# Hymba block on one core: the second half's gate in turn with the first attention's first steps, and two changes to the order of loads

## The chip, the core and the metric

The kernel runs on one core of a Trainium2 chip. The metric is the device time of one execution in microseconds (us): 2039.54 us as the median of three executions of the kernel before (2036.24, 2039.54 and 2040.94). The engines named below are TensorE (PE: matrix products and transposes; its weight loads are listed apart as PEld), VectorE (DVE: adds, subtractions, scans, multiplications), ScalarE (ACT: copies and functions such as exp), GpSimd (POOL, hardly used here) and SyncE (SP), whose queue issues nearly all of the transfers (DMAs) between device memory and the core's own memory.

## The reference

The block has 2048 positions of width 1024. One projection makes the inputs of two mixers: gated linear attention with four heads (key width 64, value width 128) and a short convolution of width 3 over 512 columns. Their outputs are joined, projected and added to the input; a feed-forward part of inner width 2816 follows, with a normalisation ahead of each part and at the end. Cut to what matters here:

```python
proj = rmsnorm(x, norm1_g) @ w_in
p_q, p_k, p_v, p_g, p_a, c_b, c_c, c_h = split(proj)
log_a = log_sigmoid(p_a @ w_gate_up + b_gate) / 16          # the gate
# attention, chunk by chunk (b is the running sum of log_a in the chunk)
scores  = where(causal, (q * exp(b)) @ (k * exp(-b)).T, 0)
o       = scores @ v + (q * exp(b)) @ state
state   = exp(b_last) * state + (k * exp(b_last - b)).T @ v
o_gla   = rmsnorm(o, gla_norm_g) * silu(p_g)
o_conv  = c_b * causal_depthwise_conv(c_c * c_h, conv_w)
x = x + concat([o_gla, o_conv]) @ w_out
x = x + (silu(h2 @ w_ffn_gate) * (h2 @ w_ffn_up)) @ w_ffn_down    # h2 = rmsnorm(x, norm2_g)
return rmsnorm(x, norm_f_g)
```

## The kernel before

**Tiling.** The sequence is cut into four blocks `b` of 512 positions, two to a half (half 0: blocks 0 and 1). The kernel's attention chunk `t` has 128 positions, so there are four to a block and eight to a half. Tiles are 128 partitions by 512 elements of f32 in most places.

**Products.** Large products go by units. A unit (`unit`) makes a 2x2 group of output tiles from a 2x2 group of weight quarters with seven products in place of eight, in the manner of Strassen and Winograd; `S1` to `S4` are sums and differences of the weight quarters `A11`, `A12`, `A21`, `A22`, and `B11`, `T1` and so on are those of the operands. Each number is split into a high part and a low part: `split` makes the high part on ACT (line 206) and the low part on DVE (line 207). `product_step` then issues three matmuls per step: high by high (line 504), high by low (505) and low by high (506), and four or eight steps make a product. `plus` (line 538, on DVE) adds a finished product to an output tile, `copied` (line 550, on ACT) copies one out of PSUM. `all_plus` is the list of all of these adds so far.

**Weights.** A unit's raw weights come in one load of 1 MB (`raw`), into one of two buffers. `unit_weights` makes the sums at line 456. The first three units of the second half use `weights_in_step` instead: its sums stand at lines 482 (`s1 = a21 + a22`), 483 and 484 (which leaves `S2` in the raw tile), each held behind an earlier `plus`. The raw buffer is free for the next unit's load when its last quarter has been split.

**Order of stages.** `in_proj(0)`, `in_proj(1)` (twelve units), `first_out_proj` (the out projection of the first half, in four pairs of output rows `d0`, ten adds to a pair), `out_proj` (that of the second half), then the feed-forward part by halves. In `first_out_proj` the loads that the second half's out projection needs are issued as well; `build_mix` (line 1411) loads convolution outputs (`s_mix`, shown as `op` from `sm`, by `load_whole`) and attention outputs (`op` from `sgla`).

**Background.** Smaller work is written as generators whose steps lie between the products. After each product `tick` (line 284) is called: it takes one background step at every other call, and with `hasty` set one more at a call in four. `hastened(steps, n)` sets `hasty` for the first `n` steps, `chain` takes generators one after the other, and `in_turn(one, *others)` (line 297) takes a step of the others, then a step of `one`, and so on, and at the end the rest of `one`.

**The gate.** `gate(1, ops)` has five steps. The first makes the low-rank logits (32 matmuls, line 1028) and stacks them; each of the other four makes one tile `z` (two matmuls, line 1054) and runs `forget_gate` on it: four activations, one DVE operation (line 1067), four scans of 128 elements (line 1070), and DVE and ACT work after them (lines 1073 to 1076). Its result is stored to device memory (`s_d`).

**The attention.** `gla_half(half)` (line 1129) runs the eight chunks. `gla_fetch` (line 1155) issues the loads `kq` (queries and keys, 256 KB), `ee` (decays, 128 KB, from `s_d`), `vt` and `gt`. `gla_scaled` makes two exponentials of the decays on ACT (lines 1163 and 1164) and multiplies queries and keys by them on DVE (1165 and 1166). `gla_scores` makes the scores on PE (line 1176), masks them on DVE (1179) and transposes keys and values (1182 and 1185). `gla_outputs` and `gla_finish` follow one step later (`o_ps`, `kv`, and the transpose `ot` at line 1251). The loads for chunk n+1 are issued after the scores of chunk n. `gla_half(0)` runs during `in_proj(1)`; `gla_half(1)` begins there in the last units and runs on in `first_out_proj`.

**What sets the order.** Each engine runs its instructions in the order in which they were issued to it, and waits at an instruction whose inputs are not there; all behind it on that engine wait too. The order within an engine is settled when the program is built. `behind(marks)` makes the instructions inside it stand behind the mark in that order. SP's queue issues its DMAs in order as well.

Of the kernel before, what the change touches and what calls it, by code (L numbers as in the profile page):

```python
# [11 lines left out]
F32 = mybir.dt.float32  # L12
# [15 lines left out]
HEADS = 4  # L28
# [26 lines left out]
def tile_hymba_block(ctx, tc, x, xt, win, wa, wgu, wout, wffn, wdown, wdown_first, small, out):  # L55
# [57 lines left out]
    def by_chunks(name, n):  # L113
        return [dram.tile([P, PT, n, P], F32, name=f"{name}{b}") for b in range(NB)]

    s_kq, s_d, s_v, s_g = [
        by_chunks(name, n) for name, n in (("sk", 4), ("sd", 2), ("sv", 4), ("sg", 4))
    ]
    s_x1 = scratch("sx", KD)
    s_mix = [  # L120
        [dram.tile([P, PB], F32, name=f"sm{b}_{k}") for k in range(4)] for b in range(NB)
    ]
# [24 lines left out]
    def bank(name="mm"):  # L147
        return ps.tile([P, PB], F32, name=name, tag="mm")
# [4 lines left out]
    def bt(name, shape=(P, PB)):  # L153
        return bx[0].tile(list(shape), F32, name=name, tag="b")

    def load(dst, src):
        return nc.sync.dma_start(dst, src)
# [10 lines left out]
    all_plus = []  # L168

    @contextmanager  # L170
    def behind(marks):

        with ExitStack() as stack:
            for m in marks:
                stack.enter_context(tc.issue_after(m.ins))
            yield
# [26 lines left out]
    def split(src, hi, lo):  # L203
        if ordered:
            return split_in_order(src, hi, lo)
        last_hi[:] = [act.activation(hi, src, AF.Copy)]  # L206
        last_lo[:] = [dve.tensor_tensor(lo, src, hi.bitcast(F32), ALU.subtract)]  # L207
        return last_lo[0]
# [64 lines left out]
    background = []  # L273
# [23 lines left out]
    def in_turn(one, *others):  # L297

        for other in others:
            for _ in other:  # L300
                yield
                if next(one, True) is None:
                    yield
        yield from one
# [6 lines left out]
    def pause(n):  # L311
        for _ in range(n):
            yield

    def hastened(steps, n):
        hasty.append(True)
        for i, _ in enumerate(steps):
            if i == n:
                hasty.clear()
            yield  # L320
# [669 lines left out]
    def load_undivided(src):  # L990
        o = opp.tile([P, 2, PB], F32R, name="op", tag="op")
        load(o[:, 1, :].bitcast(F32), src[:])
        return o

    def load_whole(src):

        o = load_undivided(src)
        split(o[:, 1, :].bitcast(F32), o[:, 0, :], o[:, 1, :])
        return o

    def load_pair(src):
        o = opp.tile([P, 2, PB], F32R, name="op", tag="op")
        load(o[:].bitcast(F32), src[:])
        return o
# [11 lines left out]
    def gate(half, ops, mark=None):  # L1016

        a = bank("a_ps")  # L1020
        names = "B11", "T1", "B21", "B22"
        with behind([mark] if mark else []):
            for n in names:
                for k in range(4):
                    q = {"B11": 3 * k + 1, "T1": 3 * k, "B21": 2 * k + 13, "B22": 2 * k + 12}[n]
                    w = wa_sb[:, 32 * q : 32 * q + P]
                    for e in range(2):
                        pe.matmul(  # L1028
                            a[:], w, ops[n][k][:, e, :],
                            start=(n, k, e) == ("B11", 0, 0),  # L1030
                            stop=n == "B22" and k == 3 and e == 1, skip_group_check=True,
                        )
        if mark:
            yield

        stacks = []
        if half == 0:
            second_factor()
        for j in range(2):
            stack = bx[0].tile([96, PB], F32R, name="a_sb", tag="b")  # L1040
            r, low = [slice(32 * n, 32 * n + 32) for n in (j, 1 - j)]
            with behind(held):
                act.activation(stack[r, :], a[r, :], AF.Copy)
                act.activation(stack[64:96, :], a[r, :], AF.Copy)
                dve.tensor_tensor(stack[low, :], a[r, :], stack[r, :].bitcast(F32), ALU.subtract)
            stacks.append(stack)
        yield
        for j in range(2):
            small = decays[2 * half + j] = [
                mtiny.tile([P, 2, PT], F32, name=n, tag=n, bufs=4) for n in ("em", "dn", "el")  # L1050
            ]
            for i in range(2):
                z = bank("z")
                pe.matmul(
                    z[:], wgu_sb[:, i * P : (i + 1) * P], stacks[j][:], start=True, stop=True
                )
                forget_gate(2 * half + j, i, z, *small)
                yield
# [69 lines left out]
    def gla_half(half):  # L1128
        chunks = [(b, t) for b in (2 * half, 2 * half + 1) for t in range(PT)]
        with tc.issue_after(last_silu[0].ins):  # L1130
            tables = act.preload_act_table_set("natural_log_exp_and_others")
        fetched = gla_fetch(*chunks[0])
        yield
        with tc.issue_after(tables.ins):
            cur = gla_scaled(*fetched)
        yield
        o = None
        for n, (b, t) in enumerate(chunks):
            s = gla_scores(b, t, *cur)
            yield  # L1140
            if n + 1 < len(chunks):
                fetched = gla_fetch(*chunks[n + 1])
            if o is not None:
                yield from gla_finish(*chunks[n - 1], *o)
            o = gla_outputs(b, t, *s)
            if n + 1 < len(chunks):
                cur = gla_scaled(*fetched)
            yield
        yield from gla_finish(b, t, *o)
        done.add((b, t))  # L1150
        yield
# [3 lines left out]

    def gla_fetch(b, t):
        kq, e, vt, g = [bt(n, (P, 4, P)) for n in ("kq", "ee", "vt", "gt")]
        for dst, src in ((kq[:], s_kq), (e[:, 2:4, :], s_d), (vt[:], s_v), (g[:], s_g)):
            load(dst, src[b][:, t])
        return kq, e, vt, g  # L1160

# [250 lines left out]
    def build_mix():  # L1412
        def pair(b, k):
            if k < HEADS:
                return load_pair(s_gla[b][:, k])
            with behind(all_plus[-4:-3] if k < HEADS + 2 else all_plus[-2:-1]):
                return load_whole(s_mix[b][k - HEADS])

        return {k: [pair(2 + j, k) for j in range(2)] for k in LATE_HEADS}

# [411 lines left out]
    ops, raw, between, steps, rest = opening()  # L1832
# [7 lines left out]
    drain_background()  # L1840
    ops = load_pairs(s_h1)
    ahead.append(conv_operands())
    background.extend([pause(3), hastened(chain(gate(1, ops), gla_half(0)), 12)])
    in_proj(1, ops)
    drain_background(lambda: (1, PT - 1) in done)
    ssq = first_out_proj(residual(0), *mix_operands())
# [118 lines left out]
```

## Time and profile before

| | |
|---|---|
| median of three executions | 2039.54 us |
| profiled execution, its own time | 2035.4 us |
| its span (first to last instruction) | 2033.6 us |
| mean granted TensorE clock | 0.996 |
| PE busy | 2011.0 us, 99% of the span |
| DVE busy | 1566.0 us, 77% |
| ACT busy | 973.5 us, 48% |
| moved by DMA | 425.12 MB, 209 GB/s over the span |

The profiled execution is one of its own, 4.1 us under the median. Its span is the time between the first and the last instruction on the core; 1.8 us of its time lie outside. "Busy" is the share of the span in which an engine had an instruction under way, and the granted clock is the share of full TensorE speed that the chip allowed. A view by windows gives the busy time of each engine in one stretch, and the number of its instructions in brackets; the view of waits sums, for each pair of lines, the time in which one engine stood idle until the other was done; the timeline lists instructions with their start and length. Names of tiles are shown in the profile without their buffer numbers; the listing of the program's order in the next section has them, so that one tile can be followed.

### The profile page before, as it was taken

The numbers are of one execution on the slowest core, as the hardware profiler recorded it, in microseconds if no ns is written. First come the engines' busy times: TensorE is split into PE (matmuls) and PEld (weight loads), VectorE is DVE, ScalarE is ACT, GpSimd is POOL, SyncE is SP. The second block draws the span as 40 slices with busy tenths as digits, with TensorE's granted clock in tenths as the row PEclk, the third lists the DMA queues.
The fourth block names the chain that finished last, engine by engine and source line by source line (L and its number), as shares of the span: only waits on it lengthen the run. The fifth ranks groups of instructions, "written<-read, shape, count | busy, mean of one in ns | idle before, by whom it ended". The sixth has DMA issues, their size and how long they took to land.

```text
span 2033.6 us, 26792 instructions
## 1 busy us (share of the span) xinstructions
PE 2011.0 (99%) x9275; PEld 1654.9 (81%) x9275; DVE 1566.0 (77%) x2837; ACT 973.5 (48%) x1941; POOL 10.3 (1%) x17
## 2 busy tenths in 40 slices
PE   9999999999989999999999999999999999999998
PEld 8788887788878888888888888887888888888886
DVE  7878868677867877777777688887767767778886
ACT  6664465754544444444444552334434444454345
POOL 0000000000000000000000000000000000000001
PEclk9999999999999999999999999999999999999999
DMA  7366876654786863545545676486444434486653
GB/s 264 119 202 218 289 262 210 187 171 137 261 296 219 297 239 130 181 158 210 181 154 183 226 282 253 185 288 263 168 157 171 169 137 171 179 329 222 248 217 130
DMA packets 191943, 425.12 MB, mean 209 GB/s; under 512 B 17760, under 2 KB 67136, under 8 KB 182336
## 3 DMA queue, kind: packets, MB, share of 16 engines
q1 hardware_dynamic: 191088, 422.76, 59.1%
q8 instruction: 73, 1.20, 0.2%
q10 hardware_dynamic: 720, 0.66, 0.1%
q14 instruction: 62, 0.51, 0.1%
HBM read 277.60 MB, written 145.75 MB: 208 GB/s over the span
## 4 chain that ended last, share of the span: by engine, by line
PE 95%; DMA 3%; ACT 1%; DVE 1%; issue 0%; SPq 0%; POOL 0%; POOLq 0%; ACTq 0%
PE mm L504 27%; PE mm L506 27%; PE mm L505 27%; PE mm L1431 1%; PE mm L1434 1%; PE mm L1432 1%; PE mm L1393 1%; DMA op<-shT 1%; PE a_ps L1028 1%; PE mm L809 1%; PE mm L811 1%; PE mm L810 1%; PE mm L1751 1%; PE mm L1399 1%; PE o_ps L1201 1%; DMA op<-sgla 0%
## 5 line engine op out<-in xcount | busy, mean ns | idle before, releaser
L504 PE MATMUL mm<-op,wq 128*128 128x512 f32 x2499 | 973.2, 392 | 2.5 <-ACT c L550 1.2
L505 PE MATMUL mm<-op,wq 128*128 128x512 f32 x2499 | 971.8, 390 | 0.3 <-DVE op L207 0.2
L506 PE MATMUL mm<-op,wq 128*128 128x512 f32 x2499 | 961.1, 390 | 2.4 <-DVE wq L207 2.1
L206 ACT ACTIVATE wq<-raw 128x512 fp32r<-128x512 f32 (+2 forms) x628 | 361.5, 580 | 591.2 <-PE mm L506 490.8
L504 PEld LDWEIGHTS mm<-op,wq 128*128 128x128 f32 x2499 | 469.1, 188 | 104.8 <-ACT wq L206 2.4
L506 PEld LDWEIGHTS mm<-op,wq 128*128 128x128 f32 x2499 | 469.2, 188 | 101.8 <-DVE wq L207 4.1
L505 PEld LDWEIGHTS mm<-op,wq 128*128 128x128 f32 x2499 | 469.3, 188 | 97.4 <-DVE op L207 2.0
L207 DVE TENSOR_TENSOR wq<-raw,wq 128x512 fp32r<-128x512 f32 (+2 forms) x628 | 390.8, 627 | 145.4 <-ACT wq L206 144.1
L538 DVE TENSOR_TENSOR c<-mm,c 128x512 f32<-128x512 f32 x196 | 135.0, 689 | 75.5 <-PE mm L506 70.6
L538 DVE TENSOR_TENSOR y<-mm,y 128x512 f32<-128x512 f32 x185 | 126.9, 688 | 51.4 <-PE mm L506 50.7
L550 ACT ACTIVATE c<-mm 128x512 f32<-128x512 f32 x198 | 115.6, 589 | 29.5 <-PE mm L506 27.0
L456 DVE TENSOR_TENSOR raw<-raw 128x512 f32<-128x512 f32 (+2 forms) x190 | 117.0, 621 | 2.1
L206 ACT ACTIVATE wq<-s 128x512 fp32r<-128x512 f32 (+2 forms) x100 | 58.0, 580 | 110.2 <-PE mm L506 95.7
L456 DVE TENSOR_TENSOR s<-raw 128x512 f32<-128x512 f32 (+2 forms) x95 | 59.1, 622 | 31.7 <-DMA raw<-in_wffn_dram 20.8
L207 DVE TENSOR_TENSOR op<-op 128x512 fp32r<-128x512 f32 x108 | 71.1, 686 | 3.1 <-ACT op L206 3.0
L206 ACT ACTIVATE op<-op 128x512 fp32r<-128x512 f32 x108 | 63.1, 621 | 8.6 <-DMA op<-sa_T 3.5
L207 DVE TENSOR_TENSOR wq<-s,wq 128x512 fp32r<-128x512 f32 (+2 forms) x100 | 62.5, 625 | 1.8 <-ACT wq L206 1.0
L456 DVE TENSOR_TENSOR raw<-s,raw 128x512 f32<-128x512 f32 (+2 forms) x95 | 59.2, 623 | 1.3
L605 ACT ACTIVATE sg<-mm 128x512 f32<-128x512 f32 x26 | 15.5, 598 | 87.6 <-PE mm L506 87.6
L605 ACT ACTIVATE c<-c 128x512 f32<-128x512 f32 x78 | 48.9, 629 | 13.1 <-DVE c L538 10.4
L1431 PE MATMUL mm<-op,wq 128*128 128x512 f32 x128 | 50.0, 392 | 0.0
L1432 PE MATMUL mm<-op,wq 128*128 128x512 f32 x128 | 49.8, 389 | 0.0
(238 smaller groups left out, 1666.4 us busy)
## 6 DMA issues: line engine op xcount, KB each, us to landing
raw<-in_wffn_dram SPq DMA_DIRECT2D x44, 1024.0 KB, 6.6
sa_B<-so SPq DMA_DIRECT2D x47, 512.0 KB, 3.6
op<-sa_B SPq DMA_DIRECT2D x47, 512.0 KB, 6.6
raw<-in_win_dram SPq DMA_DIRECT2D x22, 1024.0 KB, 6.0
sa_T<-so SPq DMA_DIRECT2D x44, 512.0 KB, 4.3
op<-sa_T SPq DMA_DIRECT2D x44, 512.0 KB, 6.7
raw<-in_wdown_dram SPq DMA_DIRECT2D x24, 768.0 KB, 5.5
sx<-y SPq DMA_DIRECT2D x48, 256.0 KB, 3.7
```

Source lines behind the costliest of these rows:

```text
L206: last_hi[:] = [act.activation(hi, src, AF.Copy)]
L207: last_lo[:] = [dve.tensor_tensor(lo, src, hi.bitcast(F32), ALU.subtract)]
L456: dve.tensor_tensor(*args)
L504: pe.matmul(o[:], wh, xh, start=first and k == 0, stop=False, skip_group_check=True)
L505: pe.matmul(o[:], wh, xl, start=False, stop=False, skip_group_check=True)
L506: return pe.matmul(o[:], wl, xh, start=False, stop=k == n - 1, skip_group_check=True)
L538: last_plus[:] = [dve.tensor_tensor(t[:], o[:], t[:], ALU.add)]
L550: last_out[:] = [act.activation(t[:], o[:], AF.Copy)]
L605: last_silu[:] = [act.activation(s[:], c[:], AF.Silu)]
L809: pe.matmul(acc[:], wq[:, 0, c], p[:, 0, :], start=first, stop=False)
L1431: pe.matmul(o[e, j][:], wh, m[:, 0, :], start=n == 0, stop=False)
L1432: pe.matmul(o[e, j][:], wh, m[:, 1, :], start=False, stop=False)
```

## The change

There are three edits. The steps of the second half's gate and the first steps of the first half's attention are taken in turn instead of one after the other. In `gla_fetch` the decays are loaded ahead of the queries and keys. In `build_mix` the load of a convolution output is put behind the add that lies twenty adds back (two pairs of rows), and its split stays behind the add that it was behind before.

```diff
     def gla_fetch(b, t):
         kq, e, vt, g = [bt(n, (P, 4, P)) for n in ("kq", "ee", "vt", "gt")]
-        for dst, src in ((kq[:], s_kq), (e[:, 2:4, :], s_d), (vt[:], s_v), (g[:], s_g)):
+        for dst, src in ((e[:, 2:4, :], s_d), (kq[:], s_kq), (vt[:], s_v), (g[:], s_g)):
             load(dst, src[b][:, t])
         return kq, e, vt, g
...
                 return load_pair(s_gla[b][:, k])
+            with behind(all_plus[-20:-19]):
+                o = load_undivided(s_mix[b][k - HEADS])
             with behind(all_plus[-4:-3] if k < HEADS + 2 else all_plus[-2:-1]):
-                return load_whole(s_mix[b][k - HEADS])
+                split(o[:, 1, :].bitcast(F32), o[:, 0, :], o[:, 1, :])
+            return o
...
-    background.extend([pause(3), hastened(chain(gate(1, ops), gla_half(0)), 12)])
+    background.extend([pause(3), hastened(in_turn(gla_half(0), gate(1, ops)), 12)])
     in_proj(1, ops)
```

What this does to the order of the instructions shows at three places. The first is DVE in the first units of the second half, before the change, around the low part of the second unit's `S2` (`raw_3243` are that unit's weights, `wq_3255` its `S2`; `g1` and `g2` are tiles of four different runs of `forget_gate`):

```order
L484 TENSOR_TENSOR raw_3243<-s1_3245,raw_3243 128x512
L1067 SCALAR_TENSOR_TENSOR g2_3200<-g2_3200,g1_3199 128x512
L1166 SCALAR_TENSOR_TENSOR kq_3229<-kq_3229,ee_3230 128x256
L1074 TENSOR_TENSOR g2_3082<-g1_3081 128x512
L1074 TENSOR_TENSOR g2_3117<-g1_3116 128x512
L1070 SCALAR_TENSOR_TENSOR g1_3168<-ones_92,g2_3169 128x128 x4
L456 TENSOR_TENSOR s1_3479<-raw_3480 128x512
L1070 SCALAR_TENSOR_TENSOR g1_3199<-ones_92,g2_3200 128x128 x4
L207 TENSOR_TENSOR wq_3255<-raw_3243,wq_3255 128x512
L207 TENSOR_TENSOR wq_3258<-raw_3243,wq_3258 128x512
```

The same place after the change (the unit's weights are `raw_3226` now, and its `S2` is `wq_3238`):

```order
L1074 TENSOR_TENSOR g2_3174<-g1_3173 128x512
L1179 COPY_PREDICATED scores_106<-mask_94,sc_3203 128x2x128
L483 TENSOR_TENSOR raw_3226<-raw_3226 128x512
L207 TENSOR_TENSOR wq_3235<-s1_3228,wq_3235 128x512
L1076 TENSOR_TENSOR dn_3103<-em_3102,el_3104 128x4
L484 TENSOR_TENSOR raw_3226<-s1_3228,raw_3226 128x512
L456 TENSOR_TENSOR s1_3479<-raw_3480 128x512
L207 TENSOR_TENSOR wq_3238<-raw_3226,wq_3238 128x512
```

Between the row of line 484 and the low part of `S2` (line 207) there stood eight scans, two differences of line 1074 and three further operations; now one sum of the next unit's weights stands there.

The second place is DVE some products later, around the add `c22` of the same unit, before the change:

```order
L207 TENSOR_TENSOR wq_3482<-raw_3480,wq_3482 128x512
L1236 TENSOR_SCALAR hsq_3371<-hsq_3371 128x4
L456 TENSOR_TENSOR raw_3480<-s1_3479,raw_3480 128x512
L538 TENSOR_TENSOR c22_3297<-mm_3261,c22_3297 128x512
L218 TENSOR_TENSOR hl_3372<-hy_3373 128x4
L207 TENSOR_TENSOR wq_3488<-s1_3479,wq_3488 128x512
```

And after it:

```order
L207 TENSOR_TENSOR wq_3482<-raw_3480,wq_3482 128x512
L456 TENSOR_TENSOR raw_3480<-s1_3479,raw_3480 128x512
L1067 SCALAR_TENSOR_TENSOR g2_3377<-g2_3377,g1_3376 128x512
L1070 SCALAR_TENSOR_TENSOR g1_3376<-ones_92,g2_3377 128x128 x4
L1165 TENSOR_TENSOR kq_3459<-kq_3459,ee_3460 128x256
L1166 SCALAR_TENSOR_TENSOR kq_3459<-kq_3459,ee_3460 128x256
L538 TENSOR_TENSOR c22_3297<-mm_3244,c22_3297 128x512
L1074 TENSOR_TENSOR g2_3377<-g1_3376 128x512
L207 TENSOR_TENSOR wq_3488<-s1_3479,wq_3488 128x512
```

The last gate tile's operation of line 1067 and its four scans, and the two multiplications of the third chunk (number 2, `kq_3459` with its decays `ee_3460`), which wait for that chunk's loads, now stand ahead of the add.

The third place is SP's queue at the first rows of the first half's out projection, as the difference between the two programs (`sk`, `sd`, `sv` and `sg` are the stored keys and queries, decays, values and output gates; `sm` the stored convolution outputs; `sgla` the attention's):

```order
 L157 DMA y_5832<-in_xt_dram 128x512
 L163 DMA sm2_3_172<-c11_5110 128x512
+L157 DMA ee_5748<-sd3_120 128x256
 L157 DMA kq_5747<-sk3_116 128x512
-L157 DMA ee_5748<-sd3_120 128x256
 L157 DMA vt_5749<-sv3_124 128x512
 L157 DMA raw_5937<-in_wout_dram 128x2048
 L163 DMA sgla2_193<-gt_5266 512x1x128
 L157 DMA gt_5750<-sg3_128 128x512
```

The decays have moved one place forward, past the queries and keys, and nothing else in the piece has moved. The loads `op` from `sm` stand in front of it and behind it, at the same places as before. The edit in `build_mix` taken alone moves no row on any engine: its mark is an add on DVE, and the load is an instruction of SP's queue.

## The prediction

> **What bounds the kernel now.** I read first the page's head and its engines' busy time, then the waits of PE, then the chain of waits around each large one, then the timeline of each engine and the windows there.
>
> ```profile
> span 2033.6 us, 26792 instructions
> PE 2011.0 (99%) x9275; PEld 1654.9 (81%) x9275; DVE 1566.0 (77%) x2837; ACT 973.5 (48%) x1941; POOL 10.3 (1%) x17
> ...
> PE sc L1176 <- DVE kq L1166: 6.2, 1, 6.2
> PE rb_ps L1719 <- ACT rep L1710: 2.3, 2, 1.7
> PE mm L506 <- DVE wq L207: 2.1, 1, 2.1
> ```
>
> The columns of the last three rows are the sum, the count and the longest of the waits. TensorE bounds the kernel: only 2033.6 − 2011.0 = 22.6 us of the span is left in which it stands. The change takes no matmul away and adds none, so it can win only from those 22.6 us, or from the clock. Two single waits, 6.2 and 2.1 us, are the largest; the change moves work near both. The third row lies in the feed-forward part, which the change leaves alone.
>
> The 2.1 us lie in the second half's first units:
>
> ```profile
> 308.34 0.39 PE L505 MATMUL mm<-op,wq 128*128 128x512 f32 x1
> 308.72 0.50 PE L506 MATMUL mm<-op,wq 128*128 128x512 f32 x1
> ...
> 315.80 0.50 PE L506 MATMUL mm<-op,wq 128*128 128x512 f32 x1 [2.14 <-DVE wq L207]
> ...
> 309.18 0.69 DVE L484 TENSOR_TENSOR raw<-s,raw 128x512 f32<-128x512 f32 x1
> ...
> 311.93 1.37 DVE L1070 TENSOR_TENSOR_SCAN g<-ones,g 128x128 f32<-128x128 f32 x4
> ...
> 313.79 1.37 DVE L1070 TENSOR_TENSOR_SCAN g<-ones,g 128x128 f32<-128x128 f32 x4
> 315.07 1.87 DVE L207 TENSOR_TENSOR wq<-raw,wq 128x512 fp32r<-128x512 f32 x3
> ...
> 309.91 1.68 ACT L206 ACTIVATE wq<-raw 128x512 fp32r<-128x512 f32 x3 [0.51 <-DVE raw L484]
> ...
> 313.00:316.00 3.00, 0.86 (x5) 0.43 (x4) 3.00 (x8) 1.18 (x4) 0.00 (x0) 1.00 0.94 224
> ```
>
> `S2` is ready at 309.87 on DVE, and its high part starts on ACT at 309.91; a third of that row's 1.68 us makes it ready at about 310.5. Its low part starts only at 315.07: DVE is busy for all of the 3 us of the window with what stands ahead of it, eight of the gate's scans among it. PE's next low weight is that tile. The last row is a window: each engine's busy time with its instructions in brackets (PE, PEld, DVE, ACT, POOL), then the granted clock, the DMA share and GB/s. The clock stays at 1.00, so the gap costs its length and no more.
>
> The 6.2 us lie where the first half's out projection starts its pairs, at the scores of a later chunk:
>
> ```profile
> 571.00 0.61 PE L1399 MATMUL mm<-op,wq 128*128 128x512 f32 x2
> 577.78 1.22 PE L1176 MATMUL sc<-kq 64*128 64x128 f32 x8 [6.17 <-DVE kq L1166]
> ...
> 570.31 0.32 SPq L157 DMA_DIRECT2D kq<-sk  x1
> 570.92 0.32 SPq L157 DMA_DIRECT2D ee<-sd  x1
> ...
> kq<-sk SPq DMA_DIRECT2D x1, 256.0 KB, 5.2
> ...
> ee<-sd SPq DMA_DIRECT2D x1, 128.0 KB, 5.5
> ...
> 576.40 0.42 ACT L1163 ACTIVATE ee<-ee 128x256 f32<-128x256 f32 x1 [0.72 <-DMA ee<-sd]
> 576.85 0.42 ACT L1164 ACTIVATE ee<-ee 128x256 f32<-128x256 f32 x1
> ...
> 576.85 0.43 DVE L1165 TENSOR_TENSOR kq<-kq,ee 128x256 f32<-128x256 f32 x1 [1.23 <-ACT ee L1163]
> 577.30 0.42 DVE L1166 SCALAR_TENSOR_TENSOR kq<-kq,ee 128x256 f32<-128x256 f32 x1
> ...
> 540.00:571.00 31.00, 31.00 (x177) 25.20 (x176) 25.50 (x62) 13.45 (x44) 0.00 (x0) 1.00 1.03 397
> 571.00:578.00 7.00, 0.83 (x5) 0.41 (x5) 4.62 (x11) 4.47 (x10) 0.00 (x0) 0.78 1.03 377
> 578.00:582.00 4.00, 4.00 (x19) 3.44 (x20) 1.51 (x4) 0.98 (x2) 0.00 (x0) 0.54 1.07 378
> 582.00:586.00 4.00, 4.00 (x20) 3.26 (x19) 0.85 (x2) 2.10 (x4) 0.00 (x0) 1.00 1.01 377
> ```
>
> The chain is: decays issued at 570.92, landed 5.5 us later at 576.4, exponential, two multiplications, scores at 577.78. The queries and keys were there by 570.31 + 5.2 = 575.5. The transfers are the limit (DMA share 1.03 for 31 us ahead of it). Here the clock drops: 7 × 0.22 + 4 × 0.46 = 3.4 us of full-speed work are missing, which at half clock is a stretch of 6.8 us, of which 0.22/0.5 would begin at 574.9 and end at 581.7. Some 3.9 us of it lie behind the restart at 577.78 and cost 1.95 us of time beyond the gap.
>
> **The gate taken in turn.** No instruction is removed. The order of the program shows that no scan stands any more between `S2` and its low part; one 0.69 us sum of the next unit does. The low part would then end near 309.87 + 0.69 + 0.69 = 311.3, and PE wants it at 313.66 (315.80 less the 2.14). So the whole 2.14 goes, and with it 0.15 in the same unit, where two matmuls that start 0.38 apart stand against a usual 0.23 (nine of them from 329.08 to 331.21, by the two rows below): −2.29. Bounds: 0, if the scans only hold another split up, and −2.29. I take the lower, since DVE has 2.3 us to spare there.
>
> The scans go ahead of it and behind it, and bring a new wait. Now the third chunk's multiplications stand on DVE in front of the add `c22` (line 538) of this unit, and they wait for that chunk's loads; the unit's last product (line 504) waits for that add. SP issues those loads directly behind the next unit's 1 MB of raw weights, which go when the last split out of its buffer is done:
>
> ```profile
> 321.49 1.29 DVE L207 TENSOR_TENSOR wq<-raw,wq 128x512 fp32r<-128x512 f32 x2
> ...
> 322.81 0.34 SPq L157 DMA_DIRECT2D raw<-in_win_dram  x1
> ...
> 326.39 0.62 SPq L157 DMA_DIRECT2D kq<-sk  x1
> 327.11 0.40 SPq L157 DMA_DIRECT2D ee<-sd  x1
> ...
> kq<-sk SPq DMA_DIRECT2D x1, 256.0 KB, 6.1
> ...
> 329.08 0.48 PE L504 MATMUL mm<-op,wq 128*128 128x512 f32 x1
> ...
> 331.21 0.39 PE L504 MATMUL mm<-op,wq 128*128 128x512 f32 x1
> ...
> L538 DVE TENSOR_TENSOR c<-mm,c 128x512 f32<-128x512 f32 x196 | 135.0, 689 | 75.5 <-PE mm L506 70.6
> ```
>
> Before, the raw load went at 322.81, 0.03 us after the split; with PE 2.29 earlier that is 320.5. The decays follow 0.4 later and the queries and keys 0.7 after them, by the distances in these rows: 321.6. They land 6.1 us on (the slowest such transfer of this half) at 327.7, two multiplications (0.85 by the rows at 576.85 and 577.30) and the add (0.69) end at 329.2. PE comes to that product, by its place among the matmuls, where before it was at 331.21, 2.29 earlier and some 0.3 later for a transpose that is moved ahead of it: 329.2. So it is even: 0 by this count. Were the raw load no earlier than before, the add would be ready at 331.5, +2.3; were the chunk's loads no earlier than the 326.39 of before, its second transfer would land at 327.11 + 6.1 = 333.2 and the add end at 334.8, +5.6. Nothing below zero: a wait gives nothing. I take +0.3, near the first, because the split that frees the buffer depends on PE and DVE, which both come sooner.
>
> **The decays first.** Sixteen chunks are affected; only at the one with the 6.17 us gap does a fetch hold PE. SP issues both loads 0.6 us apart in either order, and as the transfers share what is saturated, the last of the two should land at 576.4 again. But the last is now the queries and keys, and the exponential (0.42) and its hand-over run while they come, so that the first multiplication starts at 576.4 instead of 576.85: −0.43. Bounds: 0, if the larger transfer, being second, lands that much later; −0.9, if they land as far apart as before (575.5). I take −0.43. The cover is the transfer itself: at a chunk whose loads are early, nothing depends on it.
>
> The clock after it: 1.95 us could go altogether (−1.95), or all 3.4 us of the lost work could fall behind the restart (+1.45). I take 0, for the gap left is 6.17 − 0.43 = 5.7 us, nearer to the 6.17 that dropped than to the 2.14 that didn't.
>
> [...]
>
> **The convolution outputs' loads.** This edit moves no instruction, its mark being on DVE's queue and the load on SP's: 0, with nothing to hide. Had it moved two pairs of such loads (four, 1 MB by 256 KB each) from in front of the chunk's loads to behind them, it would have freed 1 MB at 377 GB/s, 2.8 us; I give that nothing.
>
> **Sum.** −2.29 + 0.3 − 0.43 + 0 = −2.4 us. Against the profiled execution of 2035.4 (span 2033.6 and 1.8 outside it) this is 2033.0. That execution lies 4.1 below the median of the runs, so I set the difference against the median: 2039.54 − 2.4 = 2037.1.
>
> **The rivals.**
>
> First, *the clock comes back*. [...] −2.29 − 0.43 − 1.95 and no new wait: −4.7, 2034.9.
>
> Second, *the wait is only moved*. PE gains 2.29 and then stands 2.3 at the unit's last product, since the raw weights' buffer comes free no sooner than at 322.81. For it: the scans of the last gate tile and the chunk's multiplications all stand ahead of the add now; against it: the split that frees the buffer stands ahead of those. −0.4, 2039.1.
>
> Third, on the other side, *the add waits for the chunk's loads in full*. The fetch, one chunk further on in the queue than DVE can afford, goes as late as 326.39 as before; the add stands 5.6 us, and such a gap drops the clock as the 6.17 did (1.95). −2.29 − 0.43 + 5.6 + 1.95 = +4.8, 2044.3. It decides from a wait of 2.7 us, that is from a raw load later than 323.2. For it: stores of the gate's results and of the values stand on the same queue and wait for DVE. Against it: the last of the gate's stores and both stores of values that stood ahead of these loads stand behind them now.
>
> Fourth, *nothing reaches the end*: what is gained by 320 is lost where the transfers are saturated, since the chunk's loads there come in their own time behind 31 us of full queues: 2039.5. Against it: that stretch is filled by PE's own advance, which comes 2 us sooner too.
>
> **How the numbers follow.** Forecast 0.44; the clock comes back 0.22; the wait moved 0.12; the add waits in full 0.14; nothing reaches the end 0.08. 0.2% is 4.1 us here, about what a measurement of this kernel can tell from no change. The median of before (2039.54) stands above three quarters of the executions known (2035.4, 2036.24, 2039.54, 2040.94, mean 2038.0), so a measurement under 2035.4 needs less than the sums say: I give faster all of the first rival's 0.22 and a third of the forecast's, 0.36 in all; slower is the third rival and a few hundredths of the rest, 0.18; within 0.2% is what is left, 0.46. The range goes from 3 us under the first rival, where an execution like the lowest of before would land, 2031.5, to a little under the third, 2043.0. The forecast's own range is 2034.5 to 2039.5.
>
> **What would show it.** In the waits of PE, that of line 506 for DVE's line 207 should be gone, and on DVE no scan should stand between `S2`'s sum and its low part. A new wait of line 504 for DVE's line 538 near 327 to 330 would show the price of the new order; over 2.7 us it makes the third rival true. The wait of the scores should be 5.7 us, and the two windows after it at 0.78 and 0.54 again; both at 1.00 is the first rival. SP should issue the loads from `sm` at the same places. A gain over 3 us without a change of the clock, or a loss without a wait of line 504 or of the scores that has grown, would prove this reasoning wrong.

## The result, and the profile after

The changed kernel took 2033.82 us (median of 22 executions, 2032.23 to 2038.21) against 2037.62 us for the kernel before (22 executions, 2034.19 to 2042.61): a ratio of 0.9984, 95% interval 0.9978 to 0.999, so 2 to 4.5 us less. Forecast were 2037.1 us and a gain of 2.4. The profiled execution took 2033.76 us, 1.6 less than that of before, so the pair of profiles shows less than half of the gain of the medians. It took the experiments to find the rest.

Two of PE's largest waits after (sum, count, longest):

```profile
PE sc L1176 <- DVE kq L1166: 5.3, 1, 5.3
...
PE mm L504 <- ACT c L550: 1.7, 3, 1.2
```

The wait of line 506 for line 207 is gone, the scores' wait is 0.8 shorter (5.34 us by the timeline, against 6.17), and no wait of line 504 for line 538 has come. One small wait has: 0.35 us of line 504 for a copy of line 550.

DVE's timeline after, at the second unit's `S2` and, later, at the add of `c22`:

```profile
307.61 0.69 DVE L484 TENSOR_TENSOR raw<-s,raw 128x512 f32<-128x512 f32 x1
308.33 0.69 DVE L456 TENSOR_TENSOR s<-raw 128x512 f32<-128x512 f32 x1
308.99 0.69 DVE L207 TENSOR_TENSOR wq<-raw,wq 128x512 fp32r<-128x512 f32 x1
...
326.62 0.43 DVE L1165 TENSOR_TENSOR kq<-kq,ee 128x256 f32<-128x256 f32 x1 [0.78 <-ACT ee L1164]
326.97 0.42 DVE L1166 SCALAR_TENSOR_TENSOR kq<-kq,ee 128x256 f32<-128x256 f32 x1
327.30 0.69 DVE L538 TENSOR_TENSOR c<-mm,c 128x512 f32<-128x512 f32 x1
```

One sum instead of eight scans stands between line 484 and the low part, which is done at 309.68. The add `c22` ends at 327.99, behind the chunk's two multiplications.

SP's timeline at the same place:

```profile
319.47 0.33 SPq L157 DMA_DIRECT2D raw<-in_win_dram  x1
319.85 0.44 SPq L157 DMA_DIRECT2D ee<-sd  x1
```

And PE's:

```profile
320.93 0.39 PE L505 MATMUL mm<-op,wq 128*128 128x512 f32 x1
321.25 0.49 PE L1176 MATMUL sc<-kq 64*128 64x128 f32 x2
321.66 0.50 PE L506 MATMUL mm<-op,wq 128*128 128x512 f32 x1
...
330.74 0.39 PE L504 MATMUL mm<-op,wq 128*128 128x512 f32 x1
```

The raw weights go at 319.47, so the chunk's loads are in time, and PE, which comes to the product behind `c22` at 330.74 (nine product matmuls after the transpose, as before), doesn't wait for it. The rows at 320.93 to 321.66 show another price. Where two small matmuls of the scores lie between two of the product's, these start 0.73 us apart, 0.50 more than a product's usual step of 0.23. Before the change the eight small matmuls of a chunk's scores lay in one piece, between product matmuls at 325.13 and 326.10, and added 0.74 in all. So a piece of two cost far more here than a quarter of a piece of eight, and in the new order the scores, `o_ps` and `kv` of one early chunk stand in two pieces each.

The chain of waits at the scores after:

```profile
573.83 0.52 ACT op L206
...
574.65 0.52 ACT op L206
575.17 0.32 ACT ee L1163
575.51 0.42 DVE kq L1165
...
576.44 1.23 PE sc L1176 x8
```

And the windows there (busy of PE, PEld, DVE, ACT, POOL, then clock, DMA share, GB/s):

```profile
571.00:578.00 7.00, 1.66 (x11) 1.34 (x11) 4.42 (x11) 3.85 (x9) 0.00 (x0) 0.65 1.04 381
578.00:582.00 4.00, 4.00 (x18) 3.42 (x17) 1.37 (x5) 1.82 (x4) 0.00 (x0) 0.76 1.08 388
```

The chain no longer ends in a transfer. ACT's splits of the convolution outputs (`op`) stand ahead of the exponential, so ACT's order is now as late as the loads. The clock loses 7 × 0.35 + 4 × 0.24 = 3.4 us of full-speed work, as before.

### The profile page after: what moved, and what is told of

It reads as the page before. It is cut to its first block, busy times and chain, and to the rows that moved or that the text cites. A ratio compares the mean times of both kernels' runs of the same rounds, so it can differ in the third digit from the quotient of the medians.

```text
span 2031.9 us, 26792 instructions
## 1 busy us (share of the span) xinstructions
PE 2012.4 (99%) x9275; PEld 1655.9 (81%) x9275; DVE 1565.9 (77%) x2837; ACT 973.9 (48%) x1941; POOL 10.3 (1%) x17
## 4 chain that ended last, share of the span: by engine, by line
PE 96%; DMA 1%; ACT 1%; DVE 1%; issue 0%; SPq 0%; POOL 0%; POOLq 0%; ACTq 0%
PE mm L504 28%; PE mm L506 27%; PE mm L505 27%; PE mm L1393 1%; PE mm L1435 1%; PE mm L1437 1%; PE mm L1434 1%; DMA op<-shT 1%; PE a_ps L1028 1%; PE mm L809 1%; PE mm L811 1%; PE mm L810 1%; PE o_ps L1201 1%; PE mm L1399 1%; PE mm L1754 1%; PE sc L1176 1%
```

## The experiments

**The edits one by one.** Three runs hold one edit each: the turn, the decays first, and the tie, in this order.

```diff
-    background.extend([pause(3), hastened(chain(gate(1, ops), gla_half(0)), 12)])
+    background.extend([pause(3), hastened(in_turn(gla_half(0), gate(1, ops)), 12)])
...
-        for dst, src in ((kq[:], s_kq), (e[:, 2:4, :], s_d), (vt[:], s_v), (g[:], s_g)):
+        for dst, src in ((e[:, 2:4, :], s_d), (kq[:], s_kq), (vt[:], s_v), (g[:], s_g)):
...
+            with behind(all_plus[-20:-19]):
+                o = load_undivided(s_mix[b][k - HEADS])
             with behind(all_plus[-4:-3] if k < HEADS + 2 else all_plus[-2:-1]):
-                return load_whole(s_mix[b][k - HEADS])
+                split(o[:, 1, :].bitcast(F32), o[:, 0, :], o[:, 1, :])
+            return o
```

> The kernel before with only the gate taken in turn with the attention. Theory (the scans in front of S2's low part on DVE set the 2.14 us gap, and the interleaved order gives part of it back in switches between product matmuls and the attention's): the wait of line 506 for line 207 is gone, the gap of the scores stays at 6.0 to 6.4 us, and the median is 1.5 to 2.3 us under that of before (ratio 0.9989 to 0.9993). Rival (the whole gain of the change comes from the saturated stretch near 570 us, where an earlier start changes what the transfers do): the median falls by 3 us or more although the first gap alone is taken away, and the gap of the scores or the clock behind it changes by 1 us or more.

> The kernel before with only the decays loaded ahead of the queries and keys. Theory (a hand-over and one exponential of 0.42 us move under the transfer): the gap of the scores falls from 6.2 to 5.3 to 5.8 us, the wait of line 506 for line 207 stays at 2.1, and the median falls by 0.4 to 1.2 us (ratio 0.9994 to 0.9998). Rival (the order of the loads brings the clock back or shifts other waits): a change of 2 us or more, of either sign.

> The kernel before with only the edit in build_mix, which leaves every engine's order as it was. Theory: no change, a ratio whose interval holds 1 and a median within 1 us of before; its profile is a second look at the kernel before and shows how much a single execution differs (start, gap of the scores, clock behind it). Rival (the order that the program lists hides a change in a wait): a median that differs by more than 2 us.

Measured, against 2037.01 us for the kernel before: the turn alone 2034.66 us (ratio 0.9988, 0.9979 to 0.9997), the decays alone 2034.45 us (0.999, 0.9982 to 0.9999), the tie alone 2036.54 us (0.9997, 0.9988 to 1.0006). The tie does nothing, as its order said. The turn removes the wait and gains 2.35 us, about what was expected, with an interval of 0.6 to 4.3. The decays alone gained 2.6 us by the medians and 2.0 by the ratio, where 0.4 to 1.2 were expected; the interval, 0.2 to 3.7 us, reaches into that range, so the time by itself is no clear miss. The place is one: the first gap was to stay at 2.1 us. The waits of PE in the run with the decays alone:

```profile
PE sc L1176 <- DVE kq L1166: 5.5, 1, 5.5
...
PE mm L506 <- DVE wq L207: 0.9, 1, 0.9
```

And its timeline of DVE at the low part of `S2` shows why:

```profile
314.33 0.69 DVE L207 TENSOR_TENSOR wq<-raw,wq 128x512 fp32r<-128x512 f32 x1
314.93 1.37 DVE L1070 TENSOR_TENSOR_SCAN g<-ones,g 128x128 f32<-128x128 f32 x4
```

Loading the decays first makes a chunk's multiplications ready sooner, the builder's order on DVE shifts with that, and one tile's four scans fall behind the low part of `S2` instead of in front of it: the first gap shrinks from 2.1 to 0.9 us. Since the turn removes the whole gap, the two gains at that place don't add.

The run with the tie alone has the program of before on every engine. Its profile is a second one of the same program, and at the first gap it differs from the first. PE's timeline there:

```profile
316.66 0.50 PE L506 MATMUL mm<-op,wq 128*128 128x512 f32 x1 [2.14 <-DVE wq L207]
...
317.69 0.39 PE L504 MATMUL mm<-op,wq 128*128 128x512 f32 x1
317.92 0.59 PE L505 MATMUL mm<-op,wq 128*128 128x512 f32 x1
318.31 0.63 PE L506 MATMUL mm<-op,wq 128*128 128x512 f32 x1
318.73 0.63 PE L504 MATMUL mm<-op,wq 128*128 128x512 f32 x1
```

And the windows:

```profile
313.00:317.50 4.50, 2.36 (x18) 1.68 (x15) 4.50 (x12) 1.30 (x6) 0.00 (x0) 1.00 0.82 212
317.50:321.50 4.00, 4.00 (x12) 3.14 (x11) 4.00 (x11) 1.99 (x6) 0.00 (x0) 0.57 0.76 242
```

The gap is the same 2.14 us. But 1.3 us after it the matmuls begin to start 0.39 and then 0.42 us apart instead of 0.23, and the clock of the window is 0.57: 4 × (1 − 0.57) = 1.7 us of work are lost behind the gap. No row of PE's waits shows them.

**The first gap by itself.** One run leaves most of the gate's scans out, the other makes each twice.

```diff
-        for t in range(PT):
+        for t in range(PT if b < 2 else 1):
...
-        for t in range(PT):
+        for t in sorted(list(range(PT)) * (1 + (b > 1))):
```

> The kernel before with the second half's gate scanning only the first 128 of each 512 positions (12 of its 16 scans left out, so its decays are not the reference's). Theory (the first gap costs its 2.3 us and, in part of the executions, 1.7 us more of a dropped clock behind it, as the second profile of the program of before showed): the wait of line 506 for line 207 is gone or under 0.5 us, the clock stays at 1.00 from 310 to 325 us, the gap of the scores stays at 6 to 7 us, and the median is 2.5 to 4 us under before. Rival (the first gap is worth its length alone): 1.8 to 2.3 us under before. Rival (the gap at the scores and its clock make the difference between runs): less than 1 us, since that gap is untouched.

> The kernel before with each of the second half's sixteen scans made twice (the second writes the same values). Theory: twelve scans in place of eight stand between S2's sum and its low part, and others ahead of the sum, so the first gap grows by 1.5 to 3.5 us to about 3.5 to 5.5 us, and a gap of that length drops the clock in every execution for 3.4 us, so 1.7 us more: the median is 2.5 to 5 us above before and the profile shows a granted clock near 0.8 in the 5 us behind the gap. Rival (DVE has room and the scheduler hides the extra scans): the gap stays near 2.1 and the time within 1 us of before. Rival (the drop after the gap in the second profile had another cause): the gap grows but the clock behind it stays at 1.00.

With 12 scans left out, over the whole gate and not only in front of `S2`'s low part, the time was 2033.29 us against 2037.74 (ratio 0.9981, 0.9973 to 0.999), about 3.9 us less. The gap of the scores was 6.5 us, as long as it had been, and the clock stayed up behind the place of the first gap. The windows:

```profile
310.00:315.00 5.00, 5.00 (x31) 3.94 (x30) 5.00 (x13) 3.79 (x12) 0.00 (x0) 1.00 0.87 214
315.00:320.00 5.00, 5.00 (x32) 4.19 (x32) 4.18 (x11) 2.78 (x7) 0.00 (x0) 1.00 0.87 274
```

That is above the gap's length of 2.3 us and inside the range for gap and clock together; the interval, 2 to 5.5 us, doesn't exclude the length alone.

With the scans doubled the time was 2043.84 us, 6.1 us more (ratio 1.003, 1.0018 to 1.0042). The forecast of the time came out somewhat low and that of the place wrong: the first gap did not grow, and the extra scans held PE at another place, at a transpose 20 us later. PE's timeline there:

```profile
316.30 0.50 PE L506 MATMUL mm<-op,wq 128*128 128x512 f32 x1 [2.06 <-DVE wq L207]
...
336.07 0.47 PE L1251 MATMUL ot<-ident,osb 128*128 128x128 f32 x1 [2.58 <-DVE osb L1242]
337.20 0.63 PE L506 MATMUL mm<-op,wq 128*128 128x512 f32 x1
```

Behind the gap of 2.06 us this execution kept its clock; behind that of 2.58 us the matmuls run 0.43 apart again. A further wait of this profile, 2.3 us of line 504 for an operand's split (line 206) near 1400 us, need not come from the scans: the same wait lies between 0 and 2.6 us in the profiles of this case, 0.9 in the first one of before.

**How often the clock drops.**

Two further runs of the program of before, one profile and one time each, with nothing changed:

> The kernel before, one more profile. Theory: the first gap is 2.1 us again; the clock behind it is either 1.00 (as in the first profile) or drops for 3.4 us (as in the second), and the gap of the scores is 6 to 7 us with a drop in every case. Rival (the drop in the second profile was a chance event that does not belong to this gap): 1.00 behind the first gap in this and the next look.

> The kernel before, a further profile, with the same expectations as the look ahead of it: two more looks make four at the first gap, and the theory (a drop in about half of the executions) is in doubt if only the one that was seen shows it.

They took 2038.19 and 2037.53 us. The windows from 315 to 325 us of the one, then of the other:

```profile
315.00:320.00 5.00, 3.72 (x11) 2.97 (x12) 5.00 (x14) 1.18 (x4) 0.00 (x0) 0.76 0.80 243
320.00:325.00 5.00, 5.00 (x30) 4.03 (x29) 3.68 (x11) 3.82 (x15) 0.00 (x0) 0.90 0.47 141
```

```profile
315.00:320.00 5.00, 3.36 (x11) 2.70 (x12) 5.00 (x14) 1.25 (x4) 0.00 (x0) 0.81 0.84 236
320.00:325.00 5.00, 5.00 (x29) 4.01 (x28) 3.68 (x10) 3.68 (x13) 0.00 (x0) 0.84 0.44 133
```

Both dropped: 5 × (0.24 + 0.10) = 1.7 us and 5 × (0.19 + 0.16) = 1.75 us lost. The price shows as well in PE's own positions, which need no reading of the clock. These are the first matmul of the second half's gate (line 1028) and the scores of the fourth chunk (line 1176): of the kernel before, of the run with the tie alone, and of the changed kernel.

```profile
270.88 2.48 PE L1028 MATMUL a_ps<-op,wa_sb 128*128 128x512 f32 x10
364.26 0.72 PE L1176 MATMUL sc<-kq 64*128 64x128 f32 x8
```

```profile
271.75 1.54 PE L1028 MATMUL a_ps<-op,wa_sb 128*128 128x512 f32 x6
366.75 0.71 PE L1176 MATMUL sc<-kq 64*128 64x128 f32 x8
```

```profile
271.40 1.77 PE L1028 MATMUL a_ps<-op,wa_sb 128*128 128x512 f32 x7
363.13 0.71 PE L1176 MATMUL sc<-kq 64*128 64x128 f32 x8
```

The stretch is 93.38 us long, then 95.00, and 91.73 after the change. So the change gains 1.65 us here against the profile without a drop and 3.27 against one with it. The other two profiles gave 95.0 too, and so did the run `e9_second_gap_only` below; the first profile, from which the prediction was made, is the only one of five profiles of this front of the program that shows no drop. The changed front stands in four of the runs below as well, and there the stretch is 91.72 or 91.73 us each time, so the price of the drop is gone with the gap. With the turn alone it is 91.32, and with the decays alone, where 0.9 us of the gap are left and no drop follows, 91.99.

The traces show what goes with a drop. In the run with the tie alone the clock changes at 317.95 and at 577.37 us, 76 times 3.413 us apart, and in all 14 profiles each drop between 10 and 2010 us is 3.41 us long or twice that. So one can lay a grid of steps of 3.413 us over a trace, through the times at which its clock changes. In the first profile one of these times is 574.85, which is 76 steps behind 315.44. The two stretches of the grid at the first gap, of the first profile and then of the run with the tie alone:

```profile
312.03:315.44 3.41, 1.63 (x16) 1.07 (x12) 3.41 (x10) 1.39 (x6) 0.00 (x0) 1.00 0.75 175
315.44:318.85 3.41, 3.05 (x13) 2.55 (x14) 3.41 (x9) 0.57 (x3) 0.00 (x0) 1.00 0.91 274
```

```profile
314.54:317.95 3.41, 1.29 (x6) 1.07 (x7) 3.41 (x11) 0.89 (x3) 0.00 (x0) 1.00 0.92 242
317.95:321.36 3.41, 3.41 (x10) 2.64 (x9) 3.41 (x9) 1.85 (x6) 0.00 (x0) 0.50 0.73 229
```

In the first profile the grid cuts the gap: 3.41 − 1.63 = 1.78 us of it lie in one stretch, and the clock stays. In the second one 2.12 us lie in one stretch, and the next runs at half clock. In the other three with the gap of before it is 1.92 to 2.08 us, with a drop each; of the gaps of 2.06 and 2.58 us with the scans doubled it is 1.37, without a drop, and 1.92, with one. In all 14 profiles, between 10 and 2010 us, every stretch at full clock in which PE stood for 1.92 us or more was followed by one at half clock, and none with 1.80 us or less was. (Behind 2010 us, where the large products are done, a stretch with 1.18 us in the first profile and one with 1.07 in the changed kernel's were followed by a drop, so idle time isn't the whole measure there.) The first profile and the run with the tie alone differ in where the grid lies: the gap began 1.6 us into a stretch in the first profile, and where a stretch began in the second. Were every place equally likely, a gap of 2.14 us would put 1.9 or more into one stretch in about half of the executions, an estimate from these figures. This is read from the traces as they are; no run was made to test it.

**The second gap.** The tie of the convolution outputs' loads has no effect because it names an instruction of another engine. This run names a store on SP's own queue in its place, on top of the changed kernel:

```diff
-                    store(s_x1[j][d0 + e][:], y[e, j][:])
+                    x1_stores.append(store(s_x1[j][d0 + e][:], y[e, j][:]))
...
-            with behind(all_plus[-20:-19]):
+            with behind(x1_stores[7:8]):
                 o = load_undivided(s_mix[b][k - HEADS])
```

> The changed kernel with the tie of build_mix made effective: the convolution outputs' loads stand behind the last store of the second pair of rows, an instruction of SP's own queue, so six of them move from in front of or among the chunks' loads to the third pair. Theory (the 5.3 us gap of the scores is the time that SP's transfers ahead of the chunk's loads take): four loads of 256 KB, 1 MB at 390 GB/s, are gone ahead of the decays, the gap falls by about 2.7 us to 2.4 to 3.0, the clock behind it stays near 1.00 (1.7 to 2.0 us more), and the time is 4 to 5 us under the changed kernel's, ratio to before 0.996 to 0.9965. Rival (the loads of the attention outputs fill the freed time, or the late loads make the second half's out projection wait): the gap falls by less than 1 us or a new wait of 2 us or more stands near 660 us, and the time is within 1.5 us of the changed kernel's or above it.

It took 2032.37 us (ratio to before 0.9979, 0.997 to 0.9988), some 1 us under the changed kernel by the two ratios, where 4 to 5 were expected. The chain of waits:

```profile
573.63 0.35 DVE raw L456
574.00 0.42 ACT wq L206
574.41 0.32 ACT ee L1163
...
575.68 1.17 PE sc L1176 x8
```

The decays went 2.5 us sooner (567.01 against 569.55 in the changed kernel), near the 2.7 that was worked out. But the gap fell only by 0.9, to 4.4 us: the exponential stands on ACT behind a weight split, which waits for DVE, and that order now ends last. Transfers and the two engines' orders are nearly as late, so taking the first away alone gains little.

The next two runs move PE instead, so that the scores stand behind the 24 matmuls of the pair's second output row; the second of them has the late loads as well.

```diff
-                    if k % 2:
+                    if k % 2 if d0 else e:
                         tick()
```

> The changed kernel with the background steps of the first pair of rows moved from the first to the second output row, so that on PE the scores that wait stand behind 24 more matmuls of that pair (5.5 us of work). Theory (the 5.3 us gap is only PE standing in order at the scores): those 24 matmuls fill the gap, the wait of the scores falls below 1.5 us, the clock stays at 1.00 there, and the time falls by 5 to 7 us against the changed kernel (ratio to before 0.9949 to 0.996). Rival (the next pair's weights or the following chunk are as late, so the gap moves to them): a new wait of 2 us or more on PE between 575 and 600 us, and a gain under 3 us.

> The same with the convolution outputs' loads tied to SP's own queue as in the run before with late loads. Theory (in that run the chain behind the gap was VectorE's and ScalarE's order, not the transfers): with PE's order mended the loads' place is worth under 1 us, so the time is within 1 us of the run with the scores later alone. Rival (the transfers still end last): 2 to 3 us under it.

The scores later alone gave 2031.97 us (0.9973, 0.9963 to 0.9984), less than expected; with the late loads 2025.57 us (0.9946, 0.9933 to 0.9958), much more. In the first the gap was still 3.4 us, and 3.41 us at half clock followed it. Its ACT timeline shows what the profile's wait could not name:

```profile
574.49 0.61 ACT L206 ACTIVATE op<-op 128x512 fp32r<-128x512 f32 x1
576.51 0.42 ACT L206 ACTIVATE wq<-raw 128x256 fp32r<-128x256 f32 x1 [1.40 <-PE mm L1399]
...
577.54 0.40 ACT L1163 ACTIVATE ee<-ee 128x256 f32<-128x256 f32 x1
```

With the convolution outputs' splits in front, the exponential fell behind work that waits for PE's second row, the very matmuls that should have covered it. Without those splits it stands ahead of that row. The windows of the run with both:

```profile
571.00:576.00 5.00, 5.00 (x24) 3.98 (x22) 3.70 (x9) 2.62 (x6) 0.00 (x0) 1.00 1.01 353
576.00:582.00 6.00, 6.00 (x37) 5.03 (x37) 5.96 (x13) 4.21 (x9) 0.00 (x0) 1.00 1.07 395
```

PE stands nowhere, the clock stays at 1.00, and the DMA share is still 1 and above: with the transfers as full as before, PE has other work while they come.

**The change's worth with the second gap mended.** The last pair is that kernel once more, and the same without the turn and the decays first (the lines of both as in the kernel before):

> The kernel before with the scores later on PE and the convolution outputs' loads late, but without the gate taken in turn and without the decays first: the gap at the scores is mended, the first gap is left. Theory (the first gap costs 2.3 us and, in about half of the executions, 1.7 us of a dropped clock): the gap of the scores is gone or under 2 us, the wait of line 506 for line 207 is 2.1 again, the executions fall into two groups about 1.7 us apart, and the median lies 2.5 to 4 us above the run with all the edits. Rival (with the second gap gone the change's two edits are worth their first gap's length alone): 1.8 to 2.3 us above it and one group.

> The run with the scores later and the loads late, again, beside the run without the change's edits on the same chip. Theory: 2024.5 to 2027.5 us, no wait of PE over 1.8 us, the clock at 1.00 in all windows from 300 to 600 us. Rival (the earlier result came from a lucky phase of the clock): over 2029 us with a drop near 580 us.

2030.22 us (five executions, 2029.26 to 2033.12; ratio 0.9963, 0.995 to 0.9977) without the two edits and 2025.77 (2025.02 to 2027.35; 0.9943, 0.993 to 0.9955) with them. The two edits are 4.45 us apart by the medians, more than expected. The profile without them has the first gap with its drop. But it was the slowest of the five executions, and it also has a wait of 2.6 us of line 504 for an operand's split in the feed-forward part near 1389 us, with 3.41 us at half clock behind it: 2.6 + 1.7 = 4.3 us that the edits don't touch. That wait was 0.9 in the first profile of before and is absent in the other run. How many of the five executions had it isn't known, so the positions size the edits better: 95.01 us for the stretch without them against 91.72 with them, 3.3 us. Two groups of times 1.7 us apart can't be told from five executions. Both kernels beat the change; the one with everything is 0.9943 of the kernel before.

## Why the prediction held, and where its working didn't

The time lay in the range, the sign was right, and the gain of 2.4 us lies inside the measured interval. The forecast of 2037.1 is 3.3 us above the measured time: 1.9 of it because the median of three executions stood that much above that of 22, and 1.4 from the gain. By its steps:

- **The gate taken in turn, the gap** (forecast −2.29): the mechanism was right. The scans left the place, and the wait with them. In the state without a drop the positions show 1.65 of the 2.29. The stretch holds the same 459 matmul records before and after. Summed from the two traces, the steps between the product's and the gate's own matmuls gained about 2.4 us, and the attention's matmuls, which lie in other pieces now, cost about 0.8 more. The sum of the prediction didn't hold that term.
- **The new wait at `c22`** (forecast +0.3, range 0 to 5.6): 0. The raw load went at 319.47 where 320.5 was worked out, the add ended at 327.99 against 329.2, and PE came at 330.74 against 329.2. The third rival, slower by this wait, did not happen; nor did the second.
- **The clock at the first gap**: this is the step that failed. The prediction wrote that the clock stays at 1.00, "so the gap costs its length and no more". That was one execution, in which the grid cut the gap. In four of five profiles the gap also costs 1.7 us of halved clock behind it, so it is worth 2.3 + 0.8 × 1.7 = 3.7 us on average by those few profiles, and 3.2 if the drop comes in half of the executions. The 3.9 us of the run without most scans agree with both. It explains why the profiled pair differs by 1.6 us and the medians by 3.8: the changed front is 1.65 us shorter than in the profile without a drop, but 2.95 shorter than the mean of the five. From there to the late scores the change takes 213.31 us against 213.52 to 214.46 in the four profiles of before, 0.75 less than their mean; together that is 3.7. The prediction reckoned with a change of the clock at the second gap alone. It had named a gain over 3 us without a change of the clock as proof against itself; the gain was over 3 us, and the clock did change, at the gap where it was put at 1.00.
- **The decays first** (forecast −0.43): −0.8 at the scores in this pair of profiles, near the far bound; the gap was 5.7 to 7.1 us in the further profiles of the program of before, so one pair doesn't size it. That nothing depends on the edit at the other chunks was wrong: alone, it also took 1.2 us from the first gap by a shift in DVE's order, and the drop with them; on top of the turn it makes the front 0.4 us longer (91.73 against 91.32).
- **The clock at the second gap** (forecast 0): right, to 0.2 us; 3.4 us of full-speed work were lost before and after, and the clock was back 3.9 us behind PE's restart before (581.68) and 3.45 after (579.89). So the first rival, the clock back there, was wrong in its place: a drop did disappear, but at the first gap, and from most executions of before, not from the profiled one.
- **The convolution outputs' loads** (forecast 0): right, a ratio of 0.9997. The 2.8 us named for a tie that works was half right: the loads did go 2.5 us sooner, and 0.9 reached PE.
- **Nothing reaches the end** (rival): wrong. What PE had won by 363 us it kept, though a new wait of line 504 for line 550, 0.35 us, has come; one profile of the kernel before has that wait as well, 0.64 us long.

The prediction set the 6.17 us that dropped against the 2.14 that didn't. In the 14 profiles all eleven gaps of 3.41 to 7.08 us had a drop, but so had those of 2.56 and 2.58 us and four of 2.10 to 2.14; those of 2.06, 2.26 and one of 2.14 had none. What told the shorter ones apart was the idle time within one stretch of 3.41 us.

## What to carry to other kernels

Here a gap of 2.1 us on TensorE cost its length and, in four of five profiles with the same order at that place, 3.41 us at half clock behind it (1.7 us of work), which no wait shows. Look for such a stretch in the windows' clock or in the distance of two matmuls, and in more than one profile, for one execution can hide it. Before a gap is costed, ask how much of it can fall into one stretch between the times at which the clock can be seen to change: here 1.92 us or more in one stretch of 3.41 us had a drop behind it, 1.80 or less had none. When a late result stands in order on an engine, move the waiting instruction behind work that is ready before hastening what it waits for: here three orders were nearly equally late, each move alone gained 1.0 or 2.2 us by the ratios, and both together 7.7. A tie of the kind used here moved a load only when it named an instruction of the load's own queue.

## What the runs showed of the hardware

A gap of 2.1 us halved the clock in four of six profiles with it (five of the program's front, one with doubled scans), starting 1.3 to 1.5 us after PE had resumed and costing 1.7 us. In the first profile the clock changed between 10 us and the end at 574.85, 581.68 and 2025.52 us, 2 and then 425 steps of 3.413 us behind the first of these times; in the changed kernel's at 573.06, 579.89 and 2023.73, the same steps apart. Between 10 and 2010 us full clock was followed by half clock when PE had stood for 1.92 us or more within one such step, in all 14 profiles, and not at 1.80 us or less; the run with doubled scans has 1.80 in a gap of 2.26 us, and kept its clock. The small matmuls count as busy in these sums, as the trace lists them; whether they do for the chip was not tried. Two of the scores' small matmuls between a product's added 0.50 us of PE, eight in one piece 0.74.
